# 13 of the 20 adaLN chunks of a two-layer encoder trunk as row dot products on VectorE instead of TensorE matmuls

## The chip, the cores and the metric

The kernel runs on one core of a Trainium2 chip. The metric is device microseconds of one execution; lower is better. The core has a matrix engine (TensorE, PE in the profile; PEld are its weight loads), a vector engine (VectorE, DVE), a scalar engine (ScalarE, ACT), GpSimd (POOL, idle here after the first microseconds) and SyncE (SP), on whose queue all weight transfers from HBM are issued. Each engine takes its instructions in the order in which the program wrote them; semaphores order the engines among each other.

## What is computed

Two layers over 256 tokens of width 1024, in f32. The part that the change touches is the modulation vector of each layer, six vectors of 1024 from the condition `c`:

```python
c_act = jax.nn.silu(c)
for layer in range(DEPTH):
    mod = jnp.dot(c_act, w_mod[layer]) + b_mod[layer]          # 1024 x 6144
    sh1, sc1, g1, sh2, sc2, g2 = jnp.split(mod[:, None, :], 6, axis=-1)
    u = rms_norm(x, norm1_g[layer]) * (1.0 + sc1) + sh1
    x = x + g1 * token_mixers(u, ...)      # projections, three attentions (A, B, C), gates, w_out
    u = rms_norm(x, norm2_g[layer]) * (1.0 + sc2) + sh2
    x = x + g2 * grouped_moe(u, ...)       # 16 experts, top 2 of one group of four
return rms_norm(x, final_g)
```

`w_mod` is 1024 x 6144 for each layer, so 24 MB of weights for a single row of input. A chunk is 512 of the 6144 outputs (2 MB), a unit is 256 of them (1 MB).

## The kernel before, in words

**Stages.** For each layer: a prologue (layer 0 only), the mixers (`mixers`), the routing (`route`) and the experts (`experts`). In the trace of before the mixers of layer 0 run from about 16 to 317 us, the experts to 564, the mixers of layer 1 from 569 to 841, the experts to the end.

**Steps of the mixers.** The input projection has twelve column chunks (`ORDER`), each in two halves, so 24 steps per layer, numbered 0 to 23. A step is one half of a chunk: 24 or 48 matmuls (`by_token`, lines 590 to 592; `by_channel`, 609 to 612). Weights are split first into a high part, cast on ScalarE (L276), and a low part, subtracted on VectorE (L277), half a tile (128 x 1024) at a time; the matmuls use both. `split_to` asks for the half that is needed and for two more halves ahead (`AHEAD = 2`), which is the next step's pair: at the start of step s the program writes the splits for step s+1. In the first steps (six of layer 0, four of layer 1) the chunks run side by side.

**What else a step holds.** After the projection, `step_done` writes: rotary position work of a finished chunk (`post_rope`, L641 to L659, on VectorE, after odd steps of the chunks that need it: 5 and 7, 15 and 17), then in the order `INNER = 'FVTS'` its flips to channels (L652, PE), the values of the attention job of three steps ago (L810 on PE, L823 on VectorE), the transposes of two steps ago (L789) and the scores of this step's job (L689 on PE; softmax L745 to L779 on VectorE, with the exponentials L755 on ScalarE). Jobs run in steps 12 to 20. Steps 8 to 11 hold the indexer: scores, relu on ScalarE, weighted sum L711/L713 and sixteen rounds of top-8 (L723, L724) on VectorE.

**The modulation before.** Units 0 to 7 of layer 0 (sh1 and sc1) are dot products along rows on VectorE in the prologue and the first steps (`mod_rows`, L447: multiply a block of 128 rows of transposed `w_mod` by silu(c) spread over all partitions, and accumulate). The others are chunks on PE: `mod_matmul` (L420, eight matmuls of 32 columns in four column groups), a copy on ScalarE (L427), and a step later `mod_finish`: four transposes on PE (L434), a reduce on VectorE (L436), the bias (L457) and, for sc1 and sc2, the scale (L460). `MOD_PLAN` says which chunk stands in which step: 13 chunks in the mixers of layer 0, 6 in those of layer 1. One more (`EDGE`) stands in the routing of layer 0.

**Order.** It is written out by hand; the program's order is the queue's order. At the end of each step stand these lines:

```python
if step - 1 in mods:
    self.mod_finish(*mods[step - 1], held.pop("mod"))
if step in mods:
    held["mod"] = self.mod_copy(self.mod_matmul(*mods[step]))
```

**Transfers.** `plan` lists all weight tiles in one stream; `pump` issues the next ones on SP's queue whenever a slot is free. In the mixers the slots are six tiles of 1 MB (`raw0` to `raw5`) and a few that the attention frees late (`x0` to `x2`). A chunk takes two slots, a unit one.

Of the kernel before, what the change touches and what calls it, by code (L numbers as in the profile page):

```python
# [10 lines left out]
F32 = mybir.dt.float32  # L11
# [10 lines left out]
L = 2  # L22
D = 1024
T = 256
# [59 lines left out]
ONCES = ["gb"]  # L84

ORDER = ['gB0', 'gB1', 'bi', 'bq', 'cq', 'ck', 'cv', 'aq', 'ak', 'gC0', 'av', 'gC1']
RAW_BUFS = 6
LATE = ["x0", "x1", "x2"]
HALVES = ["h0", "h1", "h2", "h3"]
NEAR = 8  # L90


MOD_PLAN = [{5: (0, 4), 6: (0, 5), 7: (0, 6), 9: (0, 7), 11: (0, 8), 13: (0, 9), 14: (0, 10), 15: (0, 11), 17: (1, 0), 18: (1, 1), 19: (1, 2), 21: (1, 3), 22: (1, 4)}, {3: (1, 6), 5: (1, 7), 7: (1, 11), 8: (1, 10), 9: (1, 9), 14: (1, 8)}]
EDGE = {0: (1, 5)}
EDGE_AT = 7

# [51 lines left out]


class Unit:  # L150
    __slots__ = ("src", "n", "key", "tile", "slot", "halves", "block", "halved", "rows", "rest", "layer", "wide", "once")

    def __init__(self, key, src, n=512, block=None):
        self.key, self.src, self.n, self.block = key, src, n, block
        self.tile, self.slot, self.halves, self.halved = None, None, None, False
        self.rows, self.rest, self.layer, self.wide = False, None, 0, True
        self.once = False


class Kernel:  # L160
    def __init__(self, ctx, tc, a):
# [5 lines left out]
        self.stream, self.issued = [], 0  # L167
        self.slots = [f"raw{i}" for i in range(RAW_BUFS)]
        self.parts = list(HALVES)
# [32 lines left out]
    def pump(self):  # L202
        while self.issued < len(self.stream):
            u = self.stream[self.issued]
            if u.block is not None and u.block not in self.ready:
                return
            if u.rest is not None:
                self.load(u.rest, u.rest.src(), 1)
                self.issued += 1
                continue  # L210
            fits = [x for x in self.slots if u.layer <= self.l or x[0] == "r"]
            if u.once:
                fits = self.once + fits
            if not fits:
                return
            u.slot = fits[0]
            (self.once if u.slot in self.once else self.slots).remove(u.slot)
            if u.slot in ONCE:
                pool = {"gb": self.e}.get(u.slot, self.ring)
                u.tile = self.t(pool, [128, 4, 512], F32, u.slot, ONCE[u.slot])  # L220
            else:
                pool = {"uh": self.g, "ul": self.g}.get(u.slot, self.ring)
                u.tile = self.t(pool, [128, 4, 512], F32, u.slot)
            src = u.src()
            if u.rows:
                for b in range(2):
                    self.nc.sync.dma_start(u.tile[:, 2 * b:2 * b + 2], src[:, b])
            elif u.halved:
                for h in range(2 if u.halved == 2 else 1):
                    self.load(u, src, h)  # L230
            else:
                self.nc.sync.dma_start(u.tile[:, :, :u.n], src)
            self.issued += 1
# [104 lines left out]

    def cact_row(self):

        self.crow = self.t(self.w, [128, 2, 4, T], F32, "y")[:, 0].rearrange("p a b -> p (a b)")
        self.nc.sync.dma_start(self.crow[0:1], self.a["crow"])

    def fill_row(self):
# [532 lines left out]
    def mixers(self, l, parts, angles):  # L877
        nc, a = self.nc, self.a
# [116 lines left out]

        mods = MOD_PLAN[l]

# [8 lines left out]
        def step_done(step, c, h):  # L1006
            if h == 1:
                post(c)
            for what in INNER:
                act(what, step)  # L1010
            if step - 1 in mods:
                self.mod_finish(*mods[step - 1], held.pop("mod"))
            if step in mods:
                held["mod"] = self.mod_copy(self.mod_matmul(*mods[step]))

        order = list(enumerate(half_order(l)))
        if l == 0:
# [49 lines left out]
        for c in ("gA0", "gA1"):  # L1067
# [8 lines left out]
            for d in range(2):  # L1076
                k = 4 * int(c[2]) + 2 * d
# [532 lines left out]
    def plan(self):  # L1610

        a = self.a
# [7 lines left out]
        def mod(l, c):  # L1620
            for h in range(2):
                self.add(("mod", l, c, h), block("w_mod", l, c, h), split=False)

        def rows(l, i):
            u = self.add(("modt", l, i), lambda: a["w_modt"][l, 2 * i:2 * i + 2].rearrange("b p (a k) -> p b a k", a=2),
                         split=False)
            u.rows = True
            return u

        def fill(l, s):  # L1630
            if s in MOD_PLAN[l]:
                mod(*MOD_PLAN[l][s])

        def proj(l, c):
            n = COLS[c][1]
# [3 lines left out]
        for l in range(L):  # L1639
            order = list(enumerate(half_order(l)))  # L1640
            first = len(self.stream)
            if l == 0:
                for s in range(4):
                    rows(0, s).halved = 2
                    rows(0, 4 + s).halved = 2
                    for i, c in enumerate(ORDER[:N_SPLIT]):
                        n = COLS[c][1]
                        key = ("in", l, c, s // 2)
                        if s % 2 == 0:
                            u = Unit(key, block("w_in", l, c, s // 2, n), n)  # L1650
                            u.halved = 1
                            self.stream.append(u)
                        else:
                            u = Unit(("rest", *key), None)
                            u.rest = next(x for x in self.stream if x.key == key)
                            self.stream.append(u)
                            u = u.rest
# [5 lines left out]
            for s, (c, h) in order:  # L1663
                n = COLS[c][1]
                u = self.add(("in", l, c, h), block("w_in", l, c, h, n), n, split=l == 0 or s >= 2 * N_EDGE)
# [147 lines left out]
```

## Time and profile before

| | |
|---|---|
| runs, median of 3 | 1093.71 us (1092.04 to 1095.75) |
| profiled execution, its own time | 1094.52 us |
| its span | 1092.9 us |
| mean granted TensorE clock | 0.982 |
| PE busy | 1045.5 us (96% of the span) |
| VectorE busy | 553.0 us (51%) |
| ScalarE busy | 394.5 us (36%) |
| bytes read from HBM | 334.18 MB |

How to read the rows further down: times are us from the span's start, a row of a timeline gives start, duration, engine, source line, operation and tiles (out<-in); instructions of one kind that follow each other are merged (x4: four of them). In brackets stands how long the engine was idle before and who ended that. Matmuls overlap each other in their pipeline, so what one costs PE is the distance from its start to the next start. A row of a stretch gives the busy time of each engine in it, the granted clock of TensorE (1.00 is 2.4 GHz, 0.50 is 1.2 GHz), the share of the transfer engines and GB/s.

### The profile page before, as it was taken

The numbers are of one execution on the slowest core, as the hardware profiler recorded it, in microseconds if no ns is written. First come the engines' busy times: TensorE is split into PE (matmuls) and PEld (weight loads), VectorE is DVE, ScalarE is ACT, GpSimd is POOL, SyncE is SP. The second block draws the span as 40 slices with busy tenths as digits, with TensorE's granted clock in tenths as the row PEclk, the third lists the DMA queues.
The fourth block names the chain that finished last, engine by engine and source line by source line (L and its number), as shares of the span: only waits on it lengthen the run. The fifth ranks groups of instructions, "written<-read, shape, count | busy, mean of one in ns | idle before, by whom it ended". The sixth has DMA issues, their size and how long they took to land. (4 is left out here: it accounts for less than half of the span.)

```text
span 1092.9 us, 19202 instructions
## 1 busy us (share of the span) xinstructions
PE 1045.5 (96%) x7750; PEld 713.3 (65%) x7750; DVE 553.0 (51%) x1333; ACT 394.5 (36%) x746; POOL 1.5 (0%) x11
## 2 busy tenths in 40 slices
PE   7899999999999999699999999999998999979996
PEld 5779777799975343253479787879997534325344
DVE  6967767566643132122255687776664323222224
ACT  4435566654532011010245356677444111101021
POOL 0000000000000000000000000000000000000000
PEclk9999999999999999989989999999999999999997
DMA  9897776696677999999936975346766699999991
GB/s 347 342 366 306 297 264 263 227 367 254 241 270 285 381 420 420 417 419 421 406 141 251 377 288 192 118 154 232 270 232 231 220 381 420 420 419 420 420 382 38
DMA packets 53849, 336.63 MB, mean 308 GB/s; under 512 B 5617, under 2 KB 11889, under 8 KB 15474
## 3 DMA queue, kind: packets, MB, share of 16 engines
q1 hardware_dynamic: 53746, 335.25, 77.8%
q8 instruction: 65, 1.06, 0.4%
q14 instruction: 38, 0.31, 0.1%
HBM read 334.18 MB, written 1.05 MB: 307 GB/s over the span
## 5 line engine op out<-in xcount | busy, mean ns | idle before, releaser
L277 DVE TENSOR_TENSOR h<-raw,h 128x1024 fp32r<-128x1024 f32 (+1 forms) x130 | 152.5, 1214 | 60.0 <-ACT h L276 59.9
L1444 PE MATMUL mm<-raw,gb 128*32 128x512 f32 (+1 forms) x656 | 171.2, 596 | 1.1 <-DMA raw<-in_exp_w_dram 1.1
L609 PE MATMUL mm<-uh,h 128*128 128x256 f32 x480 | 139.2, 290 | 4.3 <-ACT h L276 4.3
L612 PE MATMUL mm<-uh,h 128*128 128x256 f32 x480 | 137.6, 287 | 2.2 <-DVE h L277 2.2
L611 PE MATMUL mm<-ul,h 128*128 128x256 f32 x480 | 137.0, 285 | 0.0
L276 ACT CAST h<-raw 128x1024 fp32r<-128x1024 f32 (+1 forms) x130 | 129.1, 1042 | 17.6 <-PE mm L866 7.2
L1524 DVE TENSOR_TENSOR x<-y,x 128x512 fp32r<-128x512 f32 (+1 forms) x34 | 22.5, 661 | 158.5 <-ACT x L1523 158.5
L609 PEld LDWEIGHTS mm<-uh,h 128*128 128x128 f32 x480 | 92.5, 193 | 13.8 <-issue 7.9
L1444 PE MATMUL mm<-x,gb 128*32 128x512 f32 (+1 forms) x312 | 94.5, 595 | 0.0
L612 PEld LDWEIGHTS mm<-uh,h 128*128 128x128 f32 x480 | 92.3, 192 | 3.2 <-DVE h L277 3.2
L611 PEld LDWEIGHTS mm<-ul,h 128*128 128x128 f32 x480 | 92.5, 193 | 0.0
L1410 DVE SCALAR_TENSOR_TENSOR xT<-y,mod,xT 128x256 f32<-128x256 f32 x128 | 53.2, 478 | 74.0 <-PE y L1535 74.0
L1444 PE MATMUL mm<-h,gb 128*32 128x512 f32 (+1 forms) x496 | 83.5, 595 | 0.4 <-DMA h<-in_exp_w_dram 0.4
L1444 PE MATMUL y<-raw,gt 128*32 128x512 f32 (+1 forms) x224 | 74.9, 594 | 0.0
L590 PE MATMUL mm<-h,uh 128*128 128x512 f32 (+1 forms) x176 | 71.1, 404 | 0.0
L592 PE MATMUL mm<-h,ul 128*128 128x512 f32 (+1 forms) x176 | 69.1, 393 | 0.0
L591 PE MATMUL mm<-h,uh 128*128 128x512 f32 (+1 forms) x176 | 69.0, 392 | 0.0
L1444 PEld LDWEIGHTS mm<-raw,gb 128*32 128x32 f32 (+1 forms) x656 | 44.1, 117 | 31.2 <-issue 26.6
L1354 ACT ACTIVATE gb<-y,mod,sc 128x256 f32<-128x256 f32 (+1 forms) x40 | 20.9, 522 | 111.7 <-DVE gb L1356 111.7
L1418 ACT COPY gt<-t 128x512 f32<-128x512 f32 x16 | 9.4, 586 | 128.0 <-PE t L1417 128.0
L1444 PE MATMUL y<-h,gt 128*32 128x512 f32 (+2 forms) x312 | 53.8, 572 | 1.3 <-ACT gt L1418 1.3
L1444 PEld LDWEIGHTS mm<-x,gb 128*32 128x32 f32 (+1 forms) x312 | 25.1, 122 | 43.3 <-issue 39.8
(319 smaller groups left out, 2069.8 us busy)
## 6 DMA issues: line engine op xcount, KB each, us to landing
raw<-in_exp_w_dram SPq DMA_DIRECT2D x78, 1024.0 KB, 13.5
raw<-in_w_in_dram SPq DMA_DIRECT2D x48, 1024.0 KB, 6.7
x<-in_exp_w_dram SPq DMA_DIRECT2D x45, 1024.0 KB, 14.1
h<-in_exp_w_dram SPq DMA_DIRECT2D x41, 1024.0 KB, 15.8
raw<-in_w_mod_dram SPq DMA_DIRECT2D x37, 1024.0 KB, 7.2
ul<-in_exp_w_dram SPq DMA_DIRECT2D x13, 1024.0 KB, 14.1
uh<-in_exp_w_dram SPq DMA_DIRECT2D x9, 1024.0 KB, 15.4
raw<-in_w_modt_dram SPq DMA_DIRECT2D x16, 512.0 KB, 7.4
```

Of the source, the lines that this page charges most:

```text
L276: nc.scalar.copy(hi[:, :, :u.n], src)
L277: nc.vector.tensor_sub(lo[:, :, :u.n], src, hi[:, :, :u.n].bitcast(F32))
L590: nc.tensor.matmul(o, uh, hi[:, k, :u.n], start=(kk == 0), stop=False)
L591: nc.tensor.matmul(o, uh, lo[:, k, :u.n], start=False, stop=False)
L592: nc.tensor.matmul(o, ul, hi[:, k, :u.n], start=False, stop=(kk == 7))
L609: nc.tensor.matmul(o, hi[:, k, cs], mh[kk], start=(kk == 0 and b % 2 == 0), stop=False, skip_group_check=True)
L611: nc.tensor.matmul(o, hi[:, k, cs], ml[kk], start=False, stop=False, skip_group_check=True)
L612: nc.tensor.matmul(o, lo[:, k, cs], mh[kk], start=False, stop=(kk == 7), skip_group_check=True)
L1354: self.nc.scalar.activation(out, src, AF.Identity, bias=shift, scale=scale)
L1410: nc.vector.scalar_tensor_tensor(self.xT[:, k + b], ps[:, T * b:T * b + T], self.mod[l][:, 5, k + b:k + b + 1], self.xT[:, k + b], op0=ALU ...
L1444: self.nc.tensor.matmul(o[c:c + step], lhs[:, c:c + step], x, start=start, stop=stop, skip_group_check=True)
L1524: self.nc.vector.tensor_sub(yl, ps, yh.bitcast(F32))
```

## The change

Of the 13 chunks in the mixers of layer 0 seven, and of the 6 in layer 1 all six, become 14 and 12 units on VectorE (`ROWS_PLAN`), each written at the end of its step, after the softmax and after `mod_finish`. Six chunks stay on PE, in steps 5, 9, 13, 17, 21 and 22 of layer 0; the one in the routing stays too. silu(c) keeps a tile of its own for the whole kernel, where before it shared one with a later tile. The transposed `w_mod` is laid out so that a unit is one transfer of 1 MB. The seventh raw slot and the silu tile take their SBUF from a smaller dynamic buffer (4096 bytes).

```diff
--- before.py
+++ after.py
@@ -84,13 +84,17 @@
 ONCES = ["gb"]
 
 ORDER = ['gB0', 'gB1', 'bi', 'bq', 'cq', 'ck', 'cv', 'aq', 'ak', 'gC0', 'av', 'gC1']
-RAW_BUFS = 6
+RAW_BUFS = 7
 LATE = ["x0", "x1", "x2"]
 HALVES = ["h0", "h1", "h2", "h3"]
 NEAR = 8
 
 
-MOD_PLAN = [{5: (0, 4), 6: (0, 5), 7: (0, 6), 9: (0, 7), 11: (0, 8), 13: (0, 9), 14: (0, 10), 15: (0, 11), 17: (1, 0), 18: (1, 1), 19: (1, 2), 21: (1, 3), 22: (1, 4)}, {3: (1, 6), 5: (1, 7), 7: (1, 11), 8: (1, 10), 9: (1, 9), 14: (1, 8)}]
+MOD_PLAN = [{5: (0, 10), 9: (0, 11), 13: (1, 0), 17: (1, 1), 21: (1, 2), 22: (1, 3)}, {}]
+
+ROWS_PLAN = [dict(zip((7, 8, 10, 12, 13, 14, 15, 16, 17, 18, 19, 20, 21, 23),
+                      [(0, i) for i in range(8, 20)] + [(1, 8), (1, 9)])),
+             dict(zip((5, 6, 7, 8, 10, 12, 13, 15, 17, 19, 21, 23), [(1, i) for i in range(12, 24)]))]
 EDGE = {0: (1, 5)}
 EDGE_AT = 7
 
@@ -148,12 +152,12 @@
 
 
 class Unit:
-    __slots__ = ("src", "n", "key", "tile", "slot", "halves", "block", "halved", "rows", "rest", "layer", "wide", "once")
+    __slots__ = ("src", "n", "key", "tile", "slot", "halves", "block", "halved", "rest", "layer", "wide", "once")
 
     def __init__(self, key, src, n=512, block=None):
         self.key, self.src, self.n, self.block = key, src, n, block
         self.tile, self.slot, self.halves, self.halved = None, None, None, False
-        self.rows, self.rest, self.layer, self.wide = False, None, 0, True
+        self.rest, self.layer, self.wide = None, 0, True
         self.once = False
 
 
@@ -222,10 +226,7 @@
                 pool = {"uh": self.g, "ul": self.g}.get(u.slot, self.ring)
                 u.tile = self.t(pool, [128, 4, 512], F32, u.slot)
             src = u.src()
-            if u.rows:
-                for b in range(2):
-                    self.nc.sync.dma_start(u.tile[:, 2 * b:2 * b + 2], src[:, b])
-            elif u.halved:
+            if u.halved:
                 for h in range(2 if u.halved == 2 else 1):
                     self.load(u, src, h)
             else:
@@ -338,7 +339,7 @@
 
     def cact_row(self):
 
-        self.crow = self.t(self.w, [128, 2, 4, T], F32, "y")[:, 0].rearrange("p a b -> p (a b)")
+        self.crow = self.t(self.g, [128, D], F32, "crow")
         self.nc.sync.dma_start(self.crow[0:1], self.a["crow"])
 
     def fill_row(self):
@@ -1012,6 +1013,8 @@
                 self.mod_finish(*mods[step - 1], held.pop("mod"))
             if step in mods:
                 held["mod"] = self.mod_copy(self.mod_matmul(*mods[step]))
+            if step in ROWS_PLAN[l]:
+                self.mod_rows(*ROWS_PLAN[l][step])
 
         order = list(enumerate(half_order(l)))
         if l == 0:
@@ -1622,14 +1625,13 @@
                 self.add(("mod", l, c, h), block("w_mod", l, c, h), split=False)
 
         def rows(l, i):
-            u = self.add(("modt", l, i), lambda: a["w_modt"][l, 2 * i:2 * i + 2].rearrange("b p (a k) -> p b a k", a=2),
-                         split=False)
-            u.rows = True
-            return u
+            return self.add(("modt", l, i), lambda: a["w_modt"][l, i].rearrange("p b (a k) -> p (b a) k", a=2), split=False)
 
         def fill(l, s):
             if s in MOD_PLAN[l]:
                 mod(*MOD_PLAN[l][s])
+            if s in ROWS_PLAN[l]:
+                rows(*ROWS_PLAN[l][s])
 
         def proj(l, c):
             n = COLS[c][1]
@@ -1781,7 +1783,7 @@
     arrays = {
         "smalls": np.concatenate([parts[n] for n in SM], axis=1),
         "crow": f["c"],
-        "w_modt": f["w_mod"].transpose(0, 2, 1).reshape(L, 48, 128, D),
+        "w_modt": f["w_mod"].transpose(0, 2, 1).reshape(L, 24, 2, 128, D).transpose(0, 1, 3, 2, 4),
         "positions": f["positions"].reshape(2, 128).T,
         "x": f["x"][0].T.reshape(KT, 128, T).transpose(1, 0, 2),
         "bias": f["c_rel_bias"][:, :, rel].transpose(0, 2, 1, 3),
@@ -1800,7 +1802,7 @@
     arrays["exp_w2"] = f["exp_w2"].reshape(L, NE, 4, 128, 2, 512).transpose(0, 1, 4, 3, 2, 5)
     arrays = {f"in_{k}_dram": np.ascontiguousarray(v) for k, v in arrays.items()}
 
-    nc = bacc.Bacc("TRN2", target_bir_lowering=False, num_devices=1)
+    nc = bacc.Bacc("TRN2", target_bir_lowering=False, num_devices=1, dynamic_dma_scratch_size=4096)
     aps = {k[3:-5]: nc.dram_tensor(k, v.shape, mybir.dt.from_np(v.dtype), kind="ExternalInput").ap()
            for k, v in arrays.items()}
     aps["out"] = nc.dram_tensor("out_0_dram", (128, KT, T), F32, kind="ExternalOutput").ap()
```

VectorE in layer 0, the end of step 15 and the start of step 16. `p` are the attention weights, `rs` their factors, `h` and `raw` the split's output and weights, `x` the values' low part. Before:

```order
L764 RECIPROCAL rs_1485<-sums_1474 128x2x2
L779 TENSOR_SCALAR p_1472<-p_1472,rs_1485 128x256 x4
L436 TENSOR_REDUCE mod_118<-t_1491 128x4
L457 TENSOR_TENSOR mod_118<-mod_118,sm_69 128x4
L277 TENSOR_TENSOR h_1515<-raw_1314,h_1515 128x1024
L277 TENSOR_TENSOR h_1530<-raw_1314,h_1530 128x1024
L823 TENSOR_TENSOR x_1135<-y_1560,x_1135 128x2x128
```

And in the changed kernel, at the same place:

```order
L765 RECIPROCAL rs_1434<-sums_1423 128x2x2
L780 TENSOR_SCALAR p_1421<-p_1421,rs_1434 128x256 x4
L448 SCALAR_TENSOR_TENSOR raw_1171,mod_124<-raw_1171,crow_71 128x1024 x2
L458 TENSOR_TENSOR mod_124<-mod_124,sm_69 128x2
L278 TENSOR_TENSOR h_1447<-raw_1245,h_1447 128x1024
L278 TENSOR_TENSOR h_1462<-raw_1245,h_1462 128x1024
L824 TENSOR_TENSOR x_1108<-y_1492,x_1108 128x2x128
```

The reduce of the chunk has gone, and two row blocks of 128x1024 with a bias stand between the softmax and the pair of splits. (All lines behind line 448 are one or more higher in the changed kernel.)

PE in layer 0 at that place, from the values of step 15 on. `t` are transposes, `y` scores, `mm` the projection of step 16. Before:

```order
L810 MATMUL y_1443<-x_1251,vB_597 64x128 x8
L789 MATMUL t_1454<-ident_96,p_1260 128x128 x4
L789 MATMUL t_1460<-ident_96,p_1260 128x128 x4
L689 MATMUL y_1466<-x_738,q_941 128x256
...
L434 MATMUL t_1491<-ident_96,modsb_1397 128x128 x4
L420 MATMUL mm_1498<-raw_1237,cact_126 32x512 x4
L420 MATMUL mm_1498<-raw_1284,cact_126 32x512 x4
L590 MATMUL mm_1513<-h_1399,uh_211 128x512
```

And in the changed kernel, one step later, where the flips stand ahead:

```order
L653 MATMUL t_1480<-ident_102,rope_1380 128x128 x4
L653 MATMUL t_1486<-ident_102,rope_1386 128x128 x4
L811 MATMUL y_1492<-x_1206,vB_599 64x128 x8
L790 MATMUL t_1503<-ident_102,p_1311 128x128 x4
L790 MATMUL t_1509<-ident_102,p_1311 128x128 x4
L690 MATMUL y_1515<-x_725,q_909 128x256
...
L591 MATMUL mm_1445<-h_1447,uh_214 128x512
```

The transposes of one chunk and the matmuls of the next have gone; after the scores the next projection follows at once.

VectorE in layer 1, steps 12 and 13, where no chunk's reduce stands in the kernel before. Before:

```order
L764 RECIPROCAL rs_9721<-sums_9710 128x2x2
L779 TENSOR_SCALAR p_9708<-p_9708,rs_9721 128x256 x4
L277 TENSOR_TENSOR h_9727<-raw_9438,h_9727 128x1024
L277 TENSOR_TENSOR h_9742<-raw_9438,h_9742 128x1024
L750 ISA p_9768,nmx_9769<-y_9762,sc_9368 128x256
```

And in the changed kernel:

```order
L765 RECIPROCAL rs_9556<-sums_9545 128x2x2
L780 TENSOR_SCALAR p_9543<-p_9543,rs_9556 128x256 x4
L448 SCALAR_TENSOR_TENSOR raw_9161,mod_125<-raw_9161,crow_71 128x1024 x2
L458 TENSOR_TENSOR mod_125<-mod_125,sm_69 128x2
L461 SCALAR_TENSOR_TENSOR sc_129<-mod_125,sm_69 128x2
L278 TENSOR_TENSOR h_9568<-raw_9297,h_9568 128x1024
L278 TENSOR_TENSOR h_9583<-raw_9297,h_9583 128x1024
L751 ISA p_9609,nmx_9610<-y_9603,sc_9244 128x256
```

A unit with its scale row has come in, and nothing has left this place.

## Rows read from the trace of the kernel before

**Rows 1.** The page: busy tenths of VectorE in 40 equal slices.
```profile
DVE  6967767566643132122255687776664323222224
```
**Rows 2.** Stretches: us; busy us (instructions) of each engine; PEclk, transfer share, GB/s.
```profile
72.20:112.50 40.30, 40.05 (x313) 32.94 (x309) 29.88 (x76) 19.12 (x27) 0.00 (x0) 1.00 0.84 335
112.50:203.50 91.00, 91.00 (x652) 67.51 (x649) 62.93 (x191) 52.94 (x132) 0.00 (x0) 1.00 0.75 281
452.00:464.00 12.00, 3.05 (x25) 0.81 (x17) 0.90 (x2) 0.00 (x0) 0.00 (x0) 0.82 1.01 413
464.00:470.00 6.00, 5.67 (x26) 5.67 (x27) 1.44 (x3) 1.13 (x2) 0.00 (x0) 0.50 1.02 418
599.50:652.30 52.80, 52.80 (x379) 42.78 (x378) 37.77 (x89) 20.78 (x30) 0.00 (x0) 1.00 0.87 338
652.30:732.30 80.00, 78.65 (x547) 62.80 (x545) 62.57 (x187) 51.46 (x128) 0.00 (x0) 1.00 0.43 159
```
**Rows 3.** Waits in 112.5:203.5 (L764's reads alike in 652.3:732.3): total us, times, longest.
```profile
DVE rs L764 <- ACT p L755: 11.9, 8, 2.3
DVE x L823 <- ACT x L822: 6.6, 3, 2.4
DVE p L750 <- PE y L689: 5.1, 3, 2.7
DVE y L696 <- PE y L689: 2.8, 3, 1.3
```
**Rows 4.** Timeline, layer 1: the split pair and the first matmul of step 13.
```profile
657.03 2.35 DVE L277 TENSOR_TENSOR h<-raw,h 128x1024 fp32r<-128x1024 f32 x2
...
659.04 0.50 PE L590 MATMUL mm<-h,uh 128*128 128x512 f32 x1
```
**Rows 5.** Timeline of PE, layer 0, steps 16 and 17: a chunk's parts.
```profile
159.68 0.66 PE L434 MATMUL t<-ident,modsb 128*128 128x128 f32 x4
...
168.99 1.92 PE L420 MATMUL mm<-raw,cact 128*32 128x512 f32 x16
170.84 0.39 PE L609 MATMUL mm<-uh,h 128*128 128x256 f32 x1
```
**Rows 6.** Timeline of VectorE, layer 0: step 15 from its pair to its reduce.
```profile
142.15 0.17 DVE L436 TENSOR_REDUCE mod<-t 128x4 f32<-128x16 f32 x1
142.35 0.16 DVE L457 TENSOR_TENSOR mod<-mod,sm 128x4 f32<-128x4 f32 x1
142.55 0.16 DVE L460 SCALAR_TENSOR_TENSOR sc<-mod,sm 128x4 f32<-128x4 f32 x1
142.63 2.36 DVE L277 TENSOR_TENSOR h<-raw,h 128x1024 fp32r<-128x1024 f32 x2
...
153.61 0.17 DVE L436 TENSOR_REDUCE mod<-t 128x4 f32<-128x16 f32 x1
```
**Rows 7.** Timeline of VectorE, first steps of layer 0: two units, the second with scale.
```profile
22.91 1.22 DVE L447 SCALAR_TENSOR_TENSOR raw<-raw,y 128x1024 f32<-128x1024 f32 x1
...
25.40 1.22 DVE L447 SCALAR_TENSOR_TENSOR raw<-raw,y 128x1024 f32<-128x1024 f32 x1
...
28.20 0.87 DVE L560 SCALAR_TENSOR_TENSOR uv<-xT,sc,t 128x256 f32<-128x256 f32 x2
```
**Rows 8.** Timelines: pair and first matmul of step 22, layer 0, then layer 1.
```profile
210.08 2.36 DVE L277 TENSOR_TENSOR h<-raw,h 128x1024 fp32r<-128x1024 f32 x2
...
213.35 0.39 PE L609 MATMUL mm<-uh,h 128*128 128x256 f32 x1
...
738.80 2.36 DVE L277 TENSOR_TENSOR h<-raw,h 128x1024 fp32r<-128x1024 f32 x2
...
740.52 0.36 PE L609 MATMUL mm<-uh,h 128*128 128x256 f32 x1
```
**Rows 9.** Waits of VectorE in 72.2:112.5, then in 599.5:652.3, for the indexer's scores.
```profile
DVE sc L711 <- ACT p L705: 4.4, 1, 4.4
...
DVE sc L711 <- ACT p L705: 6.4, 2, 4.4
```
**Rows 10.** Waits in the whole span: PE's for expert weights in raw tiles.
```profile
PE mm L1444 <- DMA raw<-in_exp_w_dram: 1.1, 2, 0.6
```

## The prediction

> **What bounds the kernel now.** I read the page's slices first, for where DVE is busy [rows 1]: five to nine tenths of the time in the two mixers (slices 1 to 12 and 21 to 30), one to four in the experts. Then the busy times by stretch [rows 2]. In the mixers' attention steps PE is busy 91.00 of 91.0 us in layer 0 (steps 12 to 20) and 78.65 of 80.0 in layer 1. So PE sets the time there, and what leaves it in the mixers comes off the end, as long as the engine that takes the work has room. That engine is DVE, and its room must be read along its queue, not as a share. In the same two stretches it is busy 62.93 and 62.57 us [rows 2], so it is idle 28.1 and 17.4 us; the reader is to see that 11.9 us of each is one kind of wait, the reciprocal L764 behind ScalarE's exponentials L755 [rows 3]. They belong to the softmax on which DVE has just worked, the queue runs in order, and no other work stands between, so that wait stays however much DVE gets to do. In layer 0 another 6.6, 5.1 and 2.8 us are waits for what PE has yet to make (L823 behind a copy of PE's output, L750 and L696 behind scores); these go as soon as DVE is late. 1.7 us is small gaps.
>
> The link between the two engines is the split of the weights (L277): PE cannot get on with a step before DVE has made the low part of its first half. DVE makes the pair for step s+1 at the start of its own step s. In layer 1 it starts the pair for step 13 at 657.03, which takes 2.35 us, so that the first half is there at 658.2, and PE begins that step at 659.04 [rows 4]: under 1 us to spare, already now.
>
> **What the change takes from PE.** A chunk on PE costs the group matmuls L420, 168.99 to the next matmul at 170.84, which is 1.85 us, and four transposes L434, busy 0.66 us with a tail that the next matmul hides, about 0.5 [rows 5]: 2.4 us. Thirteen go, seven in layer 0 and six in layer 1: 13 x 2.4 = 31 us. With them go thirteen copies on ScalarE, which bounds nothing here, and thirteen reduces on DVE: 0.5 us with a scale row behind (142.15 to 142.63), without its 0.16 us 0.3 [rows 6], some 5 us together.
>
> **What it adds to DVE.** A unit (two row blocks L447 with their accumulator reads, and the bias) runs in the prologue of the kernel before in the same form and size: 22.91 to 25.40 is 2.49 us, and with the scale row, 25.40 to 28.20, 2.80 [rows 7]. Twenty-six units, four of each layer with the scale row, are 18 x 2.49 + 8 x 2.80 = 67 us. The program puts a unit at the end of a step, behind the softmax and ahead of the next pair of splits. What is queued behind it is that pair, and who waits for the pair is PE. Step 15 of layer 0 shows what such a step is then: pair, rotary and softmax take DVE from 142.63 to 153.61 without a pause but for the exponentials [rows 6], 11.0 us, and with the unit 13.5.
>
> **The sum, layer 0.** From 112.5 to 203.5 DVE keeps 62.93 us of work and 11.9 us of waiting for exponentials. The units of steps 12 to 19 come to it (5 x 2.49 + 3 x 2.80 = 20.9), four of its six reduces go (-1.5): 94.2 us, or 95.9 with the small gaps, where it now has 91.0. So DVE is 3.2 to 4.9 us late by step 20; I take 4.9, since the small gaps are steps inside the softmax and not waits for PE. Step 20 has a unit itself, +2.8, and loses a reduce with scale, -0.5. At its end DVE has a lead now, which is used up first: the pair for step 22 starts at 210.08, its first half is there at 211.3, and PE begins at 213.35, 2.1 us later [rows 8]. Then what DVE brings into the stretch. In 72.2 to 112.5 it is busy 29.88 of 40.3 us [rows 2]; three units come (7.5), two reduces go (-0.7), and 4.4 us of its idle time is the wait for the indexer's scores [rows 9], which PE now makes earlier. If all idle time were filled, DVE would be 3.6 us early; if only that wait, 2.4 late. The rotary work of step 7 can begin about 1 us earlier, since PE is rid of the chunk of step 6; I take +0.8. Layer 0: 4.9 + 2.3 - 2.1 + 0.8 = +5.9 us.
>
> **The sum, layer 1.** 62.57 + 11.9, the units of steps 12, 13 and 15 (2.80 each) and of 17 and 19 (2.49 each), 13.4, and one reduce less (-0.5): 87.4, or 89.2 with as much of small gaps as in layer 0, against 80.0. DVE is 7.4 to 9.2 us late, and I take 9.2. Step 20 has no unit here. The lead at its end is 0.5 us (pair from 738.80, first half at 740.0, PE at 740.52) [rows 8]. In 599.5 to 652.3 DVE is busy 37.77 of 52.8 us [rows 2]; five units come (12.8), five reduces go (-1.7), and 6.4 us of the idle time is the indexer's [rows 9]: 3.9 us early if every gap is filled, 4.7 late if only these are. PE also starts step 4 about 2 us earlier, without its chunk of step 3, and the steps up to 8 begin with it; I take -1.6. Layer 1: 9.2 - 0.5 - 1.6 = +7.1 us.
>
> From step 22 on PE has the longer steps again (each layer has one unit left, or two, and no softmax), so the delays are not made good and do not grow. The sum is +13 us. The profiled execution took 1094.5 us, which makes 1107.5; it lies 0.8 us above the median of the three runs, 1093.7, so on the median 1107.
>
> **Edits at nothing.** The 7th slot lets transfers start earlier. PE waits for expert weights in raw tiles 1.1 us in the whole span [rows 10], so it can give about that, and in the mixers the wait is for DVE, not for transfers. The bytes stay: a unit of 1 MB for half of a 2 MB chunk. That silu(c) stays in a tile of its own moves no instruction. The smaller dynamic buffer matters only to a queue that uses it; I set it at 0, with a few us upward within the range. The Trainium skill, "SBUF — State Buffer", size table, calls this carve-out the ring for descriptors made in software (SWDGE); by that it is 0 too, as this kernel's transfers are issued by SP's hardware queue.
>
> **Rivals.** First, PE goes on setting the time: 1094.5 - 31 = 1063 us. It needs DVE to take 2.5 us more in nearly every attention step with its pairs still on time. For it speaks DVE's busy share of 63 in 91; against it the 11.9 us that no work fills, and the 13.5 us of step 15. Between it and mine lies the case that all bounds go the good way: 1094.5 + 3.2 + 2.3 - 2.1 - 3.6 + 7.4 - 0.5 - 3.9 = 1097. So even then there is no gain; for one, DVE's unit or its waits must be shorter than in these rows.
>
> Second, slower still: PE, made to wait, loses its clock. After 452 to 464, in which PE was busy 3.05 us of 12, the granted clock is 0.50 in 464 to 470 [rows 2], 1.2 of 2.4 GHz. DVE late by 2 to 5 us at a step leaves PE idle as long. At the lower clock matmuls take up to twice their time; most of that falls where PE would wait anyway, but in steps without rotary work PE has but 1 to 2 us to spare. If some eight such steps lose 1 to 2 us each, 8 to 16 us reach the end: 1116 to 1124. The Trainium skill, "TensorE: Matmul & The Clock Gate", Part 1, has the array fall to its half rate after idling, and so speaks against a change that puts gaps into a dense row of matmuls; the trace agrees with its 0.50. By that rule this rival would be the forecast; by the mixers' own rows, where 1.35 us idle in 80.0 went with a clock of 1.00, it is open at which gap it sets in, and I keep it as the smaller case.
>
> Third, the change does not do what it says: a unit waits at the head of DVE's queue for a 1 MB transfer that lands late, and the pairs behind it too. That adds to the delay, up to the 1125 of the second case. Seven slots hold some three steps of weights, so I give it little.
>
> **How the numbers follow.** DVE sets both mixers, 1098 to 1115 us: 0.65. The same with a falling clock or late transfers, 1115 to 1125 and beyond: 0.17. About even, 1091 to 1097, the bounds all the good way: 0.08. PE still sets the time, 1063 to 1090: 0.10. The likeliest is the first, 1107 us. The range is 1096 to 1122: it leaves out the last case, most of the even one and the upper end of the second. A measurement of this kernel can tell about 0.3% from no change, 3.3 us. Faster by more than that 0.11, within it 0.08, slower 0.81.
>
> **What would show it.** In the profile after, DVE's waits behind PE in steps 12 to 20 (L823, L750, L696, by their new lines) should be nearly gone, while the reciprocal's behind the exponentials stay at 11 to 12 us in each layer. PE should idle ahead of projection matmuls, released by DVE's split, 2 to 6 us at a time, some 44 us in all (31 + 13). Step 22 of layer 0 should begin about 6 us later than 213.4, and the second mixer be 7 us longer. A unit should take 2.5 to 2.8 us. PE without such waits would prove me wrong on the order of DVE's queue; a granted clock under 0.9 in the mixers would speak for the second rival.

## The result, and the profile after

| | before | after |
|---|---|---|
| median | 1092.99 us (4 runs) | 1102.95 us (4 runs, 1102.56 to 1103.34) |
| ratio, 95% interval | 1 | 1.0082 (1.0070 to 1.0095) |
| profiled execution, its span | 1094.52, 1092.9 us | 1103.34, 1101.7 us |
| mean granted TensorE clock | 0.982 | 0.970 |

The change makes the kernel 0.8% slower, 9 to 10 us; 1107 were predicted, within 1096 to 1122. The page of the changed kernel: busy time and, in the third line, VectorE's 40 slices; then three of its groups (busy, mean ns of one, idle before and its releaser).

```profile
span 1101.7 us, 18768 instructions
PE 1025.7 (93%) x7490; PEld 709.9 (64%) x7490; DVE 612.5 (56%) x1441; ACT 385.8 (35%) x733; POOL 1.5 (0%) x11
DVE  6969888866644232222255988877855422222224
...
L613 PE MATMUL mm<-uh,h 128*128 128x256 f32 x480 | 140.2, 292 | 8.8 <-DVE h L278 8.8
...
L592 PE MATMUL mm<-h,uh 128*128 128x512 f32 (+1 forms) x176 | 71.7, 408 | 12.4 <-DVE h L278 12.4
L448 DVE SCALAR_TENSOR_TENSOR raw<-raw,crow 128x1024 f32<-128x1024 f32 x66 | 78.1, 1219 | 1.0 <-DMA raw<-in_w_modt_dram 1.0
```

PE is busy 20 us less than before, VectorE 60 more, and PE waits behind VectorE's split (L278), which hardly occurred before. The stretches that answer to [rows 2]: layer 0 from 72.20 on (steps 7 to 11; step 7 began here 1.9 us before) and steps 12 to 20, then layer 1, steps 4 to 11 and 12 to 20:

```profile
72.20:109.70 37.50, 34.88 (x262) 31.48 (x261) 32.63 (x73) 15.35 (x23) 0.00 (x0) 0.95 0.75 291
109.70:204.70 95.00, 84.68 (x566) 64.58 (x564) 81.05 (x231) 50.00 (x128) 0.00 (x0) 0.98 0.64 243
...
594.66:651.80 57.14, 50.87 (x322) 46.41 (x321) 48.24 (x99) 21.91 (x30) 0.00 (x0) 0.94 0.65 242
651.80:742.05 90.25, 80.94 (x527) 64.19 (x525) 75.19 (x217) 50.71 (x127) 0.00 (x0) 0.96 0.47 175
```

The row from 599.50 in [rows 2] begins with step 5. Before, steps 4 to 11 of layer 1 were:

```profile
594.13:652.30 58.17, 58.17 (x408) 47.65 (x405) 39.89 (x91) 24.23 (x34) 0.00 (x0) 1.00 0.88 341
```

In the attention steps the order has turned over: PE was busy all the time in layer 0 and all but 1.4 us in layer 1, and is now idle 10.3 and 9.3 us. VectorE's waits in 109.7 to 204.7 are one row, and in 651.8 to 742.05 the same row with a single 1.2 us beside it. What stood under it in [rows 3] has gone:

```profile
DVE rs L765 <- ACT p L756: 11.9, 8, 2.3
```

VectorE's 81.05 us of work and 11.9 of waiting are 92.95 of 95.0; the rest is small gaps. One such step, layer 1, first on VectorE (reciprocal, unit, pair of step 14), then on PE (end of step 13's scores, step 14):

```profile
665.03 0.18 DVE L765 RECIPROCAL rs<-sums 128x4 f32<-128x4 f32 x1 [1.27 <-ACT p L756]
665.24 1.14 DVE L780 TENSOR_SCALAR p<-p,rs 128x256 f32<-128x256 f32 x4
666.30 1.22 DVE L448 SCALAR_TENSOR_TENSOR raw<-raw,crow 128x1024 f32<-128x1024 f32 x1
...
668.98 2.36 DVE L278 TENSOR_TENSOR h<-raw,h 128x1024 fp32r<-128x1024 f32 x2
```
```profile
665.43 0.39 PE L592 MATMUL mm<-h,uh 128*128 128x512 f32 x1
665.66 0.40 PE L593 MATMUL mm<-h,ul 128*128 128x512 f32 x1
665.98 1.13 PE L690 MATMUL y<-x,q 64*128 64x256 f32 x8
667.05 0.50 PE L591 MATMUL mm<-h,uh 128*128 128x512 f32 x1
670.26 0.78 PE L592 MATMUL mm<-h,uh 128*128 128x512 f32 x1 [2.71 <-DVE h L278]
670.84 0.63 PE L593 MATMUL mm<-h,ul 128*128 128x512 f32 x1
671.26 0.63 PE L591 MATMUL mm<-h,uh 128*128 128x512 f32 x1
```

PE's first matmul of the step needs only the high part. The second needs the low part, which VectorE begins at 668.98, behind the unit. PE stands 2.71 us. Behind the wait its matmuls start 0.42 us apart (670.84, 671.26), not 0.23 as ahead of it (665.43, 665.66): the granted clock is 0.51 from 670.26 to 673.40 and 1.00 from 664.00 to 667.05.

**Where the 8.8 us of the profiled execution are** (1103.34 - 1094.52) I read by taking the same matmul in both traces. The first of step 22 in layer 0, of layer 1, and of step 22 in layer 1, after:

```profile
220.01 0.39 PE L610 MATMUL mm<-uh,h 128*128 128x256 f32 x1
...
571.80 0.36 PE L610 MATMUL mm<-uh,h 128*128 128x256 f32 x1
...
752.00 0.37 PE L610 MATMUL mm<-uh,h 128*128 128x256 f32 x1
```

The start of layer 1 before:

```profile
569.33 0.36 PE L609 MATMUL mm<-uh,h 128*128 128x256 f32 x1
```

Against 213.35 and 740.52 [rows 8] and this row they are +6.7, +2.5 and +11.5 us. So the first mixer cost 6.7, the second 9.0, and between them 4.2 came back; at the end of the second mixer the delay is 11.5, and 2.7 came back behind it.

### The profile page after: what moved, and what is told of

Same layout as the page of the kernel before. It is cut to its first block, busy times and chain, and to the rows that moved or that the text cites. A ratio compares the mean times of both kernels' runs of the same rounds, so it can differ in the third digit from the quotient of the medians.

```text
span 1101.7 us, 18768 instructions
## 1 busy us (share of the span) xinstructions
PE 1025.7 (93%) x7490; PEld 709.9 (64%) x7490; DVE 612.5 (56%) x1441; ACT 385.8 (35%) x733; POOL 1.5 (0%) x11
## 5 line engine op out<-in xcount | busy, mean ns | idle before, releaser
L278 DVE TENSOR_TENSOR h<-raw,h 128x1024 fp32r<-128x1024 f32 (+1 forms) x132 | 154.9, 1214 | 46.8 <-ACT h L277 46.8
L1447 PE MATMUL mm<-raw,gb 128*32 128x512 f32 (+1 forms) x688 | 148.8, 595 | 0.0
L613 PE MATMUL mm<-uh,h 128*128 128x256 f32 x480 | 140.2, 292 | 8.8 <-DVE h L278 8.8
L610 PE MATMUL mm<-uh,h 128*128 128x256 f32 x480 | 141.7, 295 | 6.0 <-ACT h L277 4.3
L610 PEld LDWEIGHTS mm<-uh,h 128*128 128x128 f32 x480 | 95.1, 198 | 12.9 <-issue 6.5
L613 PEld LDWEIGHTS mm<-uh,h 128*128 128x128 f32 x480 | 94.9, 198 | 10.2 <-DVE h L278 10.2
L1447 PE MATMUL mm<-h,gb 128*32 128x512 f32 (+1 forms) x384 | 97.9, 595 | 0.0
L1447 PE MATMUL y<-raw,gt 128*32 128x512 f32 (+2 forms) x408 | 93.1, 569 | 2.0 <-ACT gt L1421 2.0
L1447 PE MATMUL mm<-x,gb 128*32 128x512 f32 (+1 forms) x400 | 90.7, 595 | 0.0
L592 PE MATMUL mm<-h,uh 128*128 128x512 f32 (+1 forms) x176 | 71.7, 408 | 12.4 <-DVE h L278 12.4
L448 DVE SCALAR_TENSOR_TENSOR raw<-raw,crow 128x1024 f32<-128x1024 f32 x66 | 78.1, 1219 | 1.0 <-DMA raw<-in_w_modt_dram 1.0
L1447 PEld LDWEIGHTS mm<-raw,gb 128*32 128x32 f32 (+1 forms) x688 | 39.0, 116 | 56.4 <-issue 53.2
L591 PE MATMUL mm<-h,uh 128*128 128x512 f32 (+1 forms) x176 | 71.9, 408 | 0.6 <-DVE rope_s L645 0.6
L1447 PE MATMUL y<-x,gt 128*32 128x512 f32 (+2 forms) x256 | 57.5, 581 | 0.0
```

The lines of the kernel that those rows point to most:

```text
L278: nc.vector.tensor_sub(lo[:, :, :u.n], src, hi[:, :, :u.n].bitcast(F32))
L448: nc.vector.scalar_tensor_tensor(v[:, b], v[:, b], 1.0, self.crow, op0=ALU.mult, op1=ALU.mult, accum_out=self.mod[l][:, j, k0 + b:k0 + b + 1])
L591: nc.tensor.matmul(o, uh, hi[:, k, :u.n], start=(kk == 0), stop=False)
L592: nc.tensor.matmul(o, uh, lo[:, k, :u.n], start=False, stop=False)
L610: nc.tensor.matmul(o, hi[:, k, cs], mh[kk], start=(kk == 0 and b % 2 == 0), stop=False, skip_group_check=True)
L613: nc.tensor.matmul(o, lo[:, k, cs], mh[kk], start=False, stop=(kk == 7), skip_group_check=True)
```

## The experiments

All ratios are against the kernel before on the same chip.

**The slot alone, and the slot taken out.** The first kernel has the changed one's 7th slot, silu tile, buffer and layout, but before's `MOD_PLAN`; the second is the changed kernel with one slot less.

```diff
+ROWS_PLAN = [{}, {}]
```
```diff
-RAW_BUFS = 7
+RAW_BUFS = 6
```

> The kernel before with the seventh slot, silu(c) kept in its own tile, the 4 KB buffer and the new layout of transposed w_mod; no chunk is moved. Theory (the units in VectorE's queue are the whole cost): 1092 to 1094 us, within 1 us of before (1093), since the slot can give about the 1.1 us that PE waits for raw tiles. Rival A (the slot is what gave about 4 us back in the experts of the changed kernel): 1088 to 1090. Rival B (the small buffer or the layout costs the time): over 1099.

> The changed kernel with six raw slots instead of seven. Theory (the slot gives about 1 us): 1103 to 1105 us. Rival A (the slot gave back 4 us in the experts): 1106 to 1108, with PE's waits for expert weights 3 to 4 us longer. Rival F (the mixers need the slot for the units, which would wait for transfers): over 1110, with waits of L448 for in_w_modt over 5 us instead of 1.0.

Measured 1088.06 us, 0.9951 (0.9934 to 0.9968), and 1108.42 us, 1.0135 (1.0114 to 1.0155). Rival A in both (the second 0.4 us over its range): the slot is worth some 5 us, with the units and without them. The second run changes the slot alone; the other small edits of the first, which were not run one by one, cost nothing that shows. In the trace of the first, from 54 us on the same matmuls lie where they lay before (within 0.2 us) up to the first experts; there it gains 1.7 us in layer 0 and 2.2 in layer 1. That place in layer 1, before and then with the slot:

```profile
863.71 1.03 PE L1444 MATMUL mm<-raw,gb 128*32 128x512 f32 x6
865.33 1.50 PE L1444 MATMUL mm<-raw,gb 128*32 128x512 f32 x12 [0.58 <-DMA raw<-in_exp_w_dram]
...
871.95 1.02 PE L1444 MATMUL mm<-h,gb 128*32 128x512 f32 x2
```
```profile
861.35 0.60 PE L1445 MATMUL mm<-x,gb 128*32 128x512 f32 x3
861.36 0.59 PE L1445 MATMUL mm<-h,gb 128*32 128x512 f32 x1
861.77 0.60 PE L1445 MATMUL mm<-x,gb 128*32 128x512 f32 x3
```

Groups of four matmuls, one for each 32 columns of the array, start 0.43 us apart. Before, the weights of the fourth had not landed at 863.71: two groups went with three matmuls (x6), and the next group started at 865.33, 1.2 us after the last instead of 0.43, so 0.75 late, where the row says 0.58 idle. The fourth stayed two groups behind to the end of the expert's weights, where its last two stand alone (x2 at 871.95): 0.86 us more. With a second, shorter wait (0.4 us idle for a tile `h`, 0.6 late) that makes the 2.2 us, for 1.0 us of idle time in the rows. The rest of the gain lies in smaller pieces later, of which 1.4 us are the last matmuls of that execution, which ran at full clock there and at half before.

**A narrow unit.** The row blocks take 64 of 1024 columns, so most of each dot product is left out.

```diff
-            nc.vector.scalar_tensor_tensor(v[:, b], v[:, b], 1.0, self.crow, ...
+            nc.vector.scalar_tensor_tensor(v[:, b, :n], v[:, b, :n], 1.0, self.crow[:, :n], ...
```

> The changed kernel with the row blocks of the mixers' 26 units cut to the first 64 of 1024 columns, so most of each dot product is left out; transfers, order and semaphores stay. Theory (VectorE's 67 us of units make PE late): with about 0.4 us for a unit VectorE has room again and PE sets the time, 1094.5 - 31 = 1063, 1060 to 1070 us; PE's waits behind the split in the mixers fall from about 19 us to under 4. Rival C (the units' transfers hold up the queue): the transfers are the same, so 1095 to 1104. Rival D (PE's gaps come from its clock and not from VectorE): 1085 to 1100.

Measured 1066.6 us, 0.9745 (0.9727 to 0.9762). With transfers and order unchanged, the time on VectorE alone makes 36 us; rivals C and D fall. PE's waits behind the split, up to step 21 of each mixer, are 0.6 and 3.0 us. This is the first rival of the prediction, seen by taking VectorE's price away. (With the slot's 5 us that rival would be 1058; about 6 us of what is left are PE's waits for ScalarE's copies in the mixers.)

**The unit in the wait for the exponentials.**

```diff
+                p, sums = scores(*jobs[step])
+                if step in ROWS_PLAN[l]:
+                    self.mod_rows(*ROWS_PLAN[l][step])
+                state[step] = self.normalise(*jobs[step], p, sums)
```

> The changed kernel with each unit of steps 12 to 20 put between the exponentials and the reciprocal of its step's softmax, where VectorE waits 1.2 to 2.3 us a step, instead of behind the softmax. Nothing is left out. Theory (the wait for the exponentials is lost only because nothing stands between): 11.9 us of waits in layer 0 and 7.2 us in layer 1 (five units) are filled, so 1103 - 19 = 1084, 1080 to 1090 us, and the waits L765 behind ScalarE fall to under 1 us at steps with a unit. Rival E (VectorE's queue is full wherever the unit stands, or later weights p make PE's transposes wait as long): 1100 to 1105.

Measured 1085.11 us, 0.9910 (0.9892 to 0.9927): as the theory has it. VectorE in step 12 of layer 1:

```profile
653.18 0.17 DVE L753 TENSOR_SCALAR nmx<-nmx 128x2 f32<-128x2 f32 x1
653.25 1.22 DVE L448 SCALAR_TENSOR_TENSOR raw<-raw,crow 128x1024 f32<-128x1024 f32 x1
...
655.94 0.17 DVE L765 RECIPROCAL rs<-sums 128x4 f32<-128x4 f32 x1
```

The reciprocal has no wait beside it any more. The waits of this kind are gone from layer 0, and 6.7 us are left in layer 1, at its four attention steps without a unit.

**The unit behind the pair.** Each unit of a step goes behind the next step's projection and its splits, ahead of that step's other work.

```diff
             next(gens[c])
+            if step - 1 in ROWS_PLAN[l]:
+                self.mod_rows(*ROWS_PLAN[l][step - 1])
             step_done(step, c, h)
```

> The changed kernel with each unit of the mixers moved behind the next step's pair of splits: the pair follows the softmax at once, the unit stands ahead of the next rotary work, values and softmax. Theory (VectorE's whole work in steps 12 to 20 sets them, wherever the unit stands in its queue): 1099 to 1105 us. Rival G (a unit costs because it stands ahead of the pair): PE gets each pair 2.5 us earlier in some ten steps in which it waits, 1085 to 1095.

Measured 1100.59 us, 1.0072 (1.0056 to 1.0089); rival G falls. In the mixers up to step 21 PE waits less behind the split, and in its place behind VectorE's rotary work, which the unit now holds up (rows `mm <- DVE rope_s L645`, 7.5 us, where the changed kernel has 2.4). Where VectorE's queue is full, standing ahead of the pair or behind it only chooses who waits.

**Idle matmuls in the waits.** `warm_pe` issues so many matmuls of the identity into a free PSUM tile behind the first matmul of a step.

```diff
+WARM = [{10: 18, 13: 8, 14: 6, 15: 6}, {7: 12, 10: 30, 13: 10, 14: 18}]
```

> The changed kernel with 6 to 30 idle 128x128 matmuls put behind the first matmul of nine steps where PE waits 1.2 to 4.5 us for the split (layer 0: 10, 13, 14, 15; layer 1: 7, 10, 13, 14), so that PE is busy in these waits and its clock need not fall behind them. Theory (VectorE sets these steps): no change, 1101 to 1105 us. Rival D (the falling clock costs several us of the loss): 1095 to 1099, with the granted clock of both mixers at 0.99.

Measured 1102.97 us, 1.0096 (1.0078 to 1.0113), as without them. The granted clock of steps 4 to 11 of layer 1 rose from 0.94 to 1.00, of 7 to 11 in layer 0 from 0.95 to 1.00, and nothing came of it. (In 12 to 20 of layer 0 it was 0.96, so the clock was not mended everywhere.) The second rival of the prediction is not what costs the time in these steps. Step 21 of layer 0, which these matmuls don't cover, is an exception (see below).

**Layer 1 alone.** `MOD_PLAN` of layer 0 as before, no units there.

> Only layer 1's six chunks become units, as in the changed kernel; layer 0 keeps its 13 chunks on PE; seven slots. Theory (each layer's loss is its own): e1's 1088 plus the 8.9 us by which the second mixer grew in the changed kernel, less up to 2 for transfers: 1094 to 1098. The prediction's own term of 7.1 would give 1095. Rival K (the loss of layer 1 was handed on from layer 0): 1086 to 1091.

Measured 1101.5 us, 1.0080 (1.0065 to 1.0096), 3.5 above the expected range; rival K falls. Its profiled execution took 1098.45, and in that trace the second mixer, from its first matmul to step 22, is 9.0 us longer than before, as in the changed kernel. The four other executions, 1101.4 to 1103.4, have no trace; what they lost there stays open.

**Units outside the attention steps.**

```diff
+ROWS_PLAN = [{7: (0, 8), 8: (0, 9), 21: (1, 8), 23: (1, 9)}, {5: (1, 12), 6: (1, 13), 7: (1, 14), 8: (1, 15), 21: (1, 16), 23: (1, 17)}]
```

> Units only outside the attention steps: in layer 0 four (steps 7, 8, 21, 23, two chunks' worth), in layer 1 six (steps 5 to 8, 21 and 23, three chunks' worth); all other chunks are back on PE. Theory (a unit costs PE's time only where VectorE has no room, which is in steps 10 to 20): five chunks leave PE, 5 x 2.4 = 12 us, and the slot gives 5, so 1093 - 17 = 1076, 1073 to 1080 us. Rival J (a unit ahead of the pair delays PE in any step): 1086 to 1092.

> The kernel with units only outside the attention steps once more, on the chip of the run with the idle matmuls, for the comparison. Theory and rival: 1079 to 1084 us as before, with the half clock behind step 10 of layer 0 in most executions.

Measured 1083.34 us, 0.9894 (0.9873 to 0.9915), and 1083.15 us on another chip: below rival J, but 7 above the theory. Of what is missing, 5.4 us lie at step 10 of layer 0 in the first of the two traces; in layer 1 PE waits 1.9 us for the split at step 7 and 2.4 at step 10. The unit of step 8 stands behind four rounds of top-8, the pair comes late, PE waits 2.6 us, and then the clock falls. The stretch behind that wait, in the first of the two, in the second, and in the kernel with the fewer idle matmuls of the next part:

```profile
98.50:104.70 6.20, 6.15 (x29) 6.15 (x30) 5.96 (x15) 0.00 (x0) 0.00 (x0) 0.50 0.94 382
```
```profile
98.50:104.70 6.20, 6.19 (x40) 6.19 (x41) 5.96 (x15) 0.00 (x0) 0.00 (x0) 0.74 0.95 386
```
```profile
98.50:104.70 6.20, 6.20 (x54) 6.02 (x54) 5.96 (x15) 0.00 (x0) 0.00 (x0) 1.00 0.93 381
```

That 2.4 us at step 10 of layer 1 had no lower clock behind it, in the first trace:

```profile
628.00:634.00 6.00, 5.99 (x51) 5.86 (x53) 5.76 (x15) 0.00 (x0) 0.00 (x0) 1.00 0.94 395
```

So the unit of step 8 found no room: by the sixteen rounds of top-8 steps 9 and 10 are as full as the attention steps already in the kernel before, VectorE busy 6.75 of 7.66 and 6.96 of 7.20 us:

```profile
89.84:97.50 7.66, 7.66 (x67) 6.14 (x65) 6.75 (x24) 5.35 (x8) 0.00 (x0) 1.00 0.45 183
97.50:104.70 7.20, 7.20 (x63) 6.71 (x60) 6.96 (x16) 2.74 (x4) 0.00 (x0) 1.00 0.65 237
```

**Idle matmuls where PE is the bound.**

```diff
+WARM = [{10: 18}, {7: 12, 10: 16}]
```
```diff
+WARM = [{10: 11}, {}]
```

> The kernel with units only outside the attention steps, and 12 to 18 idle 128x128 matmuls behind the first matmuls of the three steps where PE waits 1.9 to 2.6 us for a split (layer 0: 10; layer 1: 7 and 10). In its trace without them, PE waited 2.6 us in step 10 of layer 0 and then ran 6.2 us at a granted clock of 0.50, which put another 2.7 us behind the wait; here PE is the later engine afterwards, so it is not made good. Theory (a short wait costs twice where PE is the bound): the half clock behind step 10 goes, 1083.3 - 2.7 = 1080.6, 1078 to 1081 us, and the times lie closer together than 1079 to 1084. Rival L (that clock falls for another reason, or the idle matmuls cost as much): 1083 to 1085, spread as before.

> The kernel with units only outside the attention steps, with idle matmuls behind the first matmuls of one step alone, step 10 of layer 0, and so many (22 records of 0.11 us, 2.4 us) that they fit into its wait of 2.6 us; with more steps and 36 records they took 3.9 us there, 1.3 more than the wait. Theory (where PE is the bound afterwards, a wait is paid again as half clock behind it): the granted clock behind step 10 stays at 1.00, step 11 of layer 0 begins 1.4 to 2.7 us earlier than without them, and the time is 1083.2 less that, 1080.5 to 1082. Rival L: step 11 begins no earlier.

Measured 1086.63 us, 0.9938 (0.9924 to 0.9952): 3.5 us slower than without them on the same chip. Why is only seen in part. In its trace step 10 of layer 0 takes 11.0 us, against 11.2 and 12.6 without them: the idle matmuls took 3.9 us in a wait of 2.6, and the clock of 1.00 behind them made up for it. In layer 1 they cost 0.6 us at step 7 and 0.9 at step 10, where the clock was at 1.00 without them too. The rest lies outside the steps that have them and stays open. With fewer, 1084.3 us, 0.9916 (0.9894 to 0.9938). In its trace step 10 goes on at a clock of 1.00 (the third row above), and all that follows in the mixer lies 1.4 us earlier than in the second run without them, 2.8 earlier than in the first: in these traces the half clock behind a wait is paid where PE is the bound. In the total it does not show; six executions spread from 1080.6 to 1087.5. Inconclusive as a gain.

**Laid out by VectorE's waits.** In each layer six units between exponentials and reciprocal (three of them as single row blocks in two steps), two at steps 6 and 7, the others in VectorE's pauses behind step 20; five chunks on PE in layer 0, none in layer 1.

```diff
+BETWEEN = [{12: (0, 10, (0,)), 13: (0, 10, (1,)), 14: (0, 11), 15: (0, 12, (0,)), 16: (0, 12, (1,)), 17: (0, 13),
+            18: (0, 14, (0,)), 19: (0, 14, (1,)), 20: (0, 15)}, ...
+LATE_ROWS = [{"gA0": [(0, 20), (0, 21)], "gA1": [(0, 22), (0, 23)], "out": [(1, 0), (1, 1)]}, ...
```

> A version laid out by the waits of VectorE. In each layer six units stand between the exponentials and the reciprocal (whole ones in steps 14, 17 and 20 with waits of 2.0 to 2.3 us, single row blocks in the other six with 1.2 us), two at the ends of steps 6 and 7, four in VectorE's pauses of 5 to 6 us during the projections gA0 and gA1, in layer 0 two more in the output projection and two at steps 21 and 23; five chunks stay on PE in layer 0, none in layer 1. Theory (a unit costs only where VectorE has no wait to put it in): PE loses 14 chunks, 14 x 2.4 = 34 us, the slot gives 5 as e1 showed, so 1093 - 39 = 1054, 1053 to 1064 us, and PE's waits behind the split in the mixers are under 5 us in all. Rival H (units late in the mixers hold up the splits there, or their transfers push back the experts' weights): 1070 to 1085, with PE waiting in 230 to 310 us.

Measured 1066.54 us, 0.9758 (0.9736 to 0.9780): 26 us faster than before, 36 than the changed kernel, with more chunks moved (14 instead of 13). It is 2.5 over the expected range and 12.5 over its 1054; rival H, 1070 to 1085, falls. The attention steps of both layers run at a clock of 1.00 again (the rows begin and end within a few us of steps 12 and 20):

```profile
107.00:190.00 83.00, 80.20 (x551) 64.07 (x550) 75.77 (x211) 50.48 (x135) 0.00 (x0) 1.00 0.62 225
620.00:711.00 91.00, 87.18 (x589) 71.05 (x588) 85.18 (x238) 58.53 (x149) 0.00 (x0) 1.00 0.56 200
```

Up to step 22 the first mixer gained 16.0 us where 8 x 2.4 = 19 were taken from PE, the second 9.1 of 14.4; between them 4.6 more were gained, and behind the second 1.6 were lost again. Of the difference, PE's small waits for ScalarE's copies out of PSUM are seen in both layers (rows `t <- ACT q` and `x`, 1.3 to 1.6 us each), and in layer 1 a wait for the split at step 10 with a lower clock behind it. None of these was tested.

```profile
609.47 0.39 PE L617 MATMUL mm<-uh,h 128*128 128x256 f32 x1 [1.89 <-DVE h L282]
...
609.40:613.20 3.80, 3.73 (x19) 3.73 (x20) 3.63 (x11) 0.46 (x1) 0.00 (x0) 0.58 0.37 106
```

## Why the prediction held, point by point

**VectorE sets the attention steps: right, and in its sizes.** For layer 0 the sum had 82.3 us of work and 95.9 in all; the row has 81.05 and 95.0. For layer 1 it had 75.5 and 89.2; the row has 75.19 and 90.25. The waits for PE vanished, the 11.9 us for the exponentials stayed to the tenth. That nothing else stood between them and their reciprocal was the reason given, and the experiment that put the unit there gave 18 us back. A unit with its scale row takes 2.68 us (666.30 to 668.98), where 2.80 were taken.

**Layer 0, +5.9 said: +6.7, but by luck.** Its parts are off on both sides. PE began step 12 2.8 us earlier (109.71 against 112.47), where the sum had VectorE 0.8 late. Steps 12 to 20 took 4.0 us longer (95.0 against 91.0), where it had 4.9. What failed is the end: it had +2.3 - 2.1 = +0.2 there, and step 21 took 15.3 us (204.71 to 220.01) instead of 9.84, so +5.5. PE first waits 1.4 us for the split. Then its values wait for copies by ScalarE, which stand in ScalarE's queue behind the exponentials, and those wait for VectorE's late softmax. ScalarE, then PE:

```profile
209.42 0.37 ACT L756 ACTIVATE p<-y,nmx 128x128 f32<-128x128 f32 x1 [5.05 <-DVE nmx L746]
...
214.05 1.12 ACT L906 COPY x<-mm 128x512 f32<-128x512 f32 x2
```
```profile
214.74 1.42 PE L805 MATMUL y<-x 128*128 128x128 f32 x8 [2.52 <-ACT x L906]
...
216.65 3.44 PE L421 MATMUL mm<-raw,cact 128*32 128x512 f32 x16
220.01 0.39 PE L610 MATMUL mm<-uh,h 128*128 128x256 f32 x1
```

Behind that wait the chunk of step 21 runs at the lower clock: 3.36 us (216.65 to 220.01) at 0.54, against 1.86 us (211.49 to 213.35) at 1.00 before. VectorE began the pair of step 22 at 217.32, so its first half was there at 218.5, and PE came last: some 1.5 of the 5.5 us are the clock, by this one trace.

```profile
216.65:220.01 3.36, 3.36 (x17) 0.59 (x16) 3.29 (x8) 0.89 (x1) 0.00 (x0) 0.54 0.61 173
```

**Layer 1, +7.1 said: +9.0.** PE began step 12 there 3.0 us earlier against its layer's start, not 1.6; steps 12 to 20 took 10.3 longer, not 9.2. The term that failed is again the lead at the end: instead of 0.5 us won back, 1.7 more were lost in step 21, where PE's values wait 2.5 us for ScalarE's copies (row `y L805 <- ACT x L906`), here too behind late exponentials. (The sum's 89.2 us for layer 1 is 89.1 when added up again; nothing hangs on it.)

**PE's waits: there, but not all behind the split.** PE idles 28.5 us in the four stretches and 6.4 in the two steps 21, where some 44 were announced; its clock in the four is 0.94 to 0.98, where [rows 2] have 1.00, so part of its spare time went into slower matmuls. The prediction had all these waits released by the split. Of the waits up to step 22 it released 19.4 us, ScalarE's copies (L805, L790) 13.2 and the rotary work 2.4: VectorE's delay reaches PE by a second way too, over ScalarE's queue.

**"Edits at nothing": wrong.** The slot was put at about 1 us by [rows 10]; it gives 5. Two things failed: the row understates a wait (0.58 us idle in layer 1, 1.6 lost by it: 0.75 at once and 0.86 at the end of the expert's weights), and it names only raw tiles, while others wait at the same place (0.4 idle for `h`, 0.6 lost).

**"The delays are not made good": wrong as a whole.** 4.2 and 2.7 us came back in the experts and at the end. About 4 us of this is the slot, at the places that it also shortens without units; the rest are pieces between -2.8 and +1.6 us at which one trace runs at the lower clock, or has a gap that nothing in it explains, and the other not. That the total came near 1107 is luck, since two errors lie on opposite sides: mixers +15.7 instead of +13, slot -5 instead of 0; 15.7 - 5.4 = +10.

**The rivals.** PE as the bound: only when the unit is nearly free (1066.6) or stands in waits. The clock: it fell as that rival said, but the idle matmuls show that it cost nothing where VectorE comes last; the 1.5 us in step 21 of layer 0 are what is seen of that rival. The Trainium skill, "TensorE: Matmul & The Clock Gate", Part 1, calls the moment at which the clock changes variable from run to run of one kernel; the trace agrees (0.50 and 0.74 behind the same wait). Late transfers: L448 waited 1.0 us in the whole span.

## What to carry to other kernels

An engine's busy share says little on its room: read what its waits are for, and whether other work of its queue can stand in them. Work handed to a second engine belongs into a wait of that engine's own chain (here between the exponentials and the reciprocal), not between the chain and what the first engine waits for. A buffer slot that comes with a change is measured by itself, since a short wait for a transfer can cost more than its row says (here 2.2 us for 1.0 of idle time).

## What was unexpected of the hardware

One wait of PE of 2.6 us inside a dense row of matmuls was followed by up to 6.2 us at a clock of 0.50, which doubled its price; another of 2.4 us, at step 10 of layer 1 in the same trace, was not (1.00 in the 6 us behind it). The clock of PE can be raised by idle matmuls in such a wait, with no effect on the time as long as another engine comes last (1102.97 us with them, 1102.95 without). A late tile for the last of four matmuls that run side by side held up the groups behind it by 0.75 us and cost 0.86 more at the end, where the late one ran alone.
